# Transposing a gated product by DMA in two 16-bit planes, and moving two modulation streams to the output stages

## The chip, the cores and the metric

The kernel runs on one core of one Trainium2 chip. The metric is the device time of one execution in microseconds (us); the time before is the median of three runs. The profile is of one execution of its own, and its span is a little shorter than the time of a run.

## The reference

A backbone of two layers over 256 latent tokens and 256 context tokens, each of width 1024, in float32. Each layer is a half-step feed-forward network (FFN), a token mixer (neighbourhood attention in layer 0, a short gated convolution in layer 1) and a second half-step FFN; after each the stream is normalised. A modulation vector per sub-layer (shift, scale, gate) comes from the conditioning vector and a wide weight, `ada_w`. What matters here:

```python
def swiglu_ffn(h, w_in, w_out):
    a, u = jnp.split(h @ w_in, 2, axis=-1)
    return (jax.nn.silu(a) * u) @ w_out

def half_step_ffn(x, shift, scale, gate, w_in, w_out, g, b):
    y = swiglu_ffn(modulate(x, shift, scale), w_in, w_out)
    return post_norm_update(x, y, gate, 0.5, g, b)

m = (s_c @ ada_w[i] + ada_b[i]).reshape(B, N_MOD, 1, D)
```

`w_in` is 1024 x 5632, `w_out` is 2816 x 1024 and each of the nine vectors of a layer takes a 1024 x 1024 slice of `ada_w` (4.2 MB).

## The kernel before

**Precision.** Every float32 operand is split in two parts that TensorE reads as fp32r: ACT copies it (the high part, names that end in h) and DVE subtracts (the low part, names that end in l). A product is three matmuls: high by high, high by low, low by high (lines 160 to 167). So each weight tile costs ACT two copies of 128x512 and DVE two subtractions before TensorE (PE) can use it (`parts`, lines 207 to 214).

**The later FFNs.** The first FFN, which also takes the context tokens, has code of its own. The other three, (0,1), (1,0) and (1,1), go through `ffn` (line 825), and only the 256 latent tokens are left, in two tiles t of 128. Each FFN has two stages:

- The input stage (`panels`, line 449) has 11 panels p of 256 + 256 columns of `w_in` (the part for silu and the factor), 4 weight units per panel, each of 2 x 128 rows by 512 columns, and 2 token tiles: 88 steps of the generator. I call such a step a chunk: it is 6 matmuls of 128x512. When the last unit of a panel and a token tile is done, `done` in `gated` (line 476) runs: ACT takes the silu out of PSUM (line 478), DVE multiplies by the factor (line 479) into a tile that is called sil.
- The output stage (`out_gemm`, line 520) multiplies the transposed product by `w_out`: 2 halves n of the columns, 11 units and 2 token tiles, so 44 chunks. `order_skew` (line 493) runs token tile 1 five units behind tile 0, so five weight units are held between the two; the last FFN uses `order_last`.

**The transposition.** The output stage needs the product with the FFN's columns on the partitions. Four chunks (`G_LAG`) after a panel's second token tile, `rest` (line 482) puts four TensorE transposes of 128x128 into a PSUM bank called gT (line 487), and `finish` splits the bank into gh and gl.

**What sets the order.** TensorE runs in the order in which the program writes its instructions. `Late` (line 120) holds a function back until a number of chunks has passed, or until its value is asked for. On ACT, DVE, SP and POOL a scheduler places each instruction by a priority (its place in the program, less an offset; weight loads are 40 places ahead); each engine then runs its list strictly in order. SP issues nearly all DMAs, in one queue.

**Weight buffers.** A unit needs a raw tile (4 buffers) and a high and a low tile (5 buffers, and with `ext[0] = 3` three more, `whx` and `wlx`): eight in rotation. A buffer is free again when PE has used the unit for both token tiles.

**Background.** `stream` and `ada` (line 275) make the modulation vectors bit by bit: 16 loads of 512 KB for two vectors (tiles called ar, line 303), each followed by two DVE accumulations of 128x512 (acc, lines 294 and 296), then a bias, four small matmuls (line 327) and a store. `tick` (line 143) runs `rate` steps per chunk; `set_background(gen, rate, hold)` starts them `hold` chunks late, and `drain` runs what is left at once. The streams for the vectors (1,4) and (1,5) run beside the input stage of FFN (0,1) at 0.35 a chunk, those for (1,6) and (1,7) beside that of FFN (1,0) at 0.25, and (1,8) beside that of FFN (1,1) at 0.15.

Of the kernel before, what the change touches and what calls it, by code (L numbers as in the profile page):

```python
# [8 lines left out]

F32 = mybir.dt.float32  # L10
F32R = mybir.dt.float32r
AF = mybir.ActivationFunctionType
ALU = mybir.AluOpType
AX = mybir.AxisListType
# [2 lines left out]
P = 128  # L17
# [34 lines left out]
LT_LAG = (5, 5)  # L52
F0_LAG = (5, 5, 6, 7)
G_LAG = 4
ROPE_EARLY = 70
S_EARLY = 40
V_LAG = 1
# [6 lines left out]
ZP = ((0, 0), (1, 0), (0, 1), (0, 2), (1, 1), (1, 2))  # L64
E0 = (0,)
E2 = (0, 5, 7)
HOLD = 20


@with_exitstack  # L70
def backbone_kernel(
# [6 lines left out]
    nc = tc.nc  # L78
    sync = nc.sync
# [4 lines left out]
    sp = ctx.enter_context(tc.tile_pool(name="sp", bufs=2))  # L84
# [10 lines left out]
    def nm(s):  # L95
        uid[0] += 1
        return f"{s}_{uid[0]}"
# [370 lines left out]
    def run(gen):  # L468
        for _ in gen:
            pass  # L470

    def gated(func, finish, s):

        part, res = {}, []

        def done(p, t, bk):
            g = sp.tile([P, 256], F32, tag="s2", bufs=S2, name=nm("sil"))
            nc.scalar.activation(g, bk[:, 0:256], func)
            gate_ins[:] = [nc.vector.tensor_tensor(out=g, in0=g, in1=bk[:, 256:512], op=ALU.mult)]
            part[p, t] = g  # L480
            if t == 1:
                def rest():
                    ps = tpb(s)
                    for i in range(2):
                        g = part.pop((p, i))
                        for j in range(2):
                            nc.tensor.transpose(ps[:, j * 256 + i * P:j * 256 + (i + 1) * P], g[:, j * P:(j + 1) * P], ident)  # L487
                    return finish(p, ps)
                res.append(Late(G_LAG, rest))

        return done, res
# [330 lines left out]
            return hi[:, s:s + P], lo[:, s:s + P]  # L822
        return f

    def ffn(hTs, later, l, j, i, gm, nxt, own=()):
# [5 lines left out]
        done, gT = gated(AF.Silu, finish, "gT")  # L831
# [7 lines left out]
        drain()  # L839
# [278 lines left out]
    srow = cp.tile([24, P], F32, tag="row", name="srow")  # L1118
# [52 lines left out]

    cols = [(0, 256), (512, 768)] + [(D + n * 256, 2 * D + n * 256) for n in range(4)]
    run(panels(cols, w, hTs, lead_in(6), done, "wc"))
    g, hTs, later = sub_end(sc_w_out[0], lhs_T(yT), KC, 1, 1, 5, 1.0, (1, 6), "wo", order_late(KU))
    run(g)
    set_background(stream([(1, 8, 0)]), 0.15)
# [55 lines left out]
```

## Time and profile before

| | |
|---|---|
| time, median of 3 runs | 1262.23 us (1261.55 to 1262.94) |
| span of the profiled execution | 1259.9 us |
| PE busy | 1245.4 us, 99% |
| DVE busy | 952.5 us, 76% |
| ACT busy | 589.9 us, 47% |
| DMA | 268.6 MB, mean 213 GB/s |

The profile lists engines, groups of instructions and waits; L164 is line 164 of the kernel above. PE is TensorE's matmuls, DVE is VectorE, ACT is ScalarE, SP the engine whose queue issues DMAs. In a row of a timeline the first number is the start in us from the beginning of the span, the second how long the row's instructions took together, and xN their number; what ended the engine's idle time stands in brackets. A row of the windows has the stretch in us, the busy time of each engine with its instructions, the granted clock of TensorE (1.00 is full), the busy share of the 16 DMA engines and what they moved in GB/s.

### The profile page before, as it was taken

How to read it: one execution, taken by the hardware profiler on the slowest of the kernel's cores; microseconds unless marked ns; L12 is line 12 of the kernel's file. 1: busy time of each engine (PE TensorE's matmuls, PEld its weight loads, DVE VectorE, ACT ScalarE, POOL GpSimd, SP SyncE). 2: the span in 40 equal slices, each digit the busy share in tenths (PEclk: the TensorE clock that was granted, in tenths of full speed). 3: DMA queues.
4: the chain of work that ended last, by engine and by line, in shares of the span. 5: the costliest groups of instructions: out<-in, count | busy, mean ns of one | idle time of the engine just before them, and what ended most of it. 6: DMA issues, size and time to landing. Idle time of an engine off the chain costs nothing.

```text
span 1259.9 us, 17303 instructions
## 1 busy us (share of the span) xinstructions
PE 1245.4 (99%) x5922; PEld 1007.2 (80%) x5922; DVE 952.5 (76%) x1678; ACT 589.9 (47%) x1152; POOL 41.4 (3%) x71
## 2 busy tenths in 40 slices
PE   9999999999999999999999999999999999999997
PEld 6787778777878877877888788888788887888786
DVE  3699987888878877889898546988546788876546
ACT  2432132312326456687655435655435644655431
POOL 0000000000001011121000000000000000000000
PEclk9999999999999999999999999999999999999999
DMA  9976678878842744465899645898645764886641
GB/s 300 310 241 215 197 239 280 269 255 266 300 149 85 217 93 92 93 130 170 256 342 318 225 144 169 285 340 268 214 145 170 247 202 131 262 289 184 223 158 55
DMA packets 202776, 268.59 MB, mean 213 GB/s; under 512 B 30090, under 2 KB 149362, under 8 KB 202688
## 3 DMA queue, kind: packets, MB, share of 16 engines
q1 hardware_dynamic: 202652, 267.48, 67.3%
q8 instruction: 46, 0.75, 0.2%
q14 instruction: 42, 0.34, 0.1%
q10 hardware_dynamic: 36, 0.02, 0.0%
HBM read 265.27 MB, written 2.17 MB: 212 GB/s over the span
## 4 chain that ended last, share of the span: by engine, by line
PE 92%; DVE 3%; ACT 3%; issue 1%; DMA 0%; POOL 0%; DVEq 0%; SPq 0%; ACTq 0%; POOLq 0%
PE f L679 19%; PE w L164 17%; PE w L167 17%; PE w L165 17%; PE wkv L164 2%; PE wkv L165 2%; PE wkv L167 2%; PE wc L164 2%; PE wc L167 2%; PE wc L165 2%; PE gT L487 1%; PE ada L608 1%; PE ada L327 1%; PE S L971 1%; ACT pr L979 1%
## 5 line engine op out<-in xcount | busy, mean ns | idle before, releaser
L210 ACT ACTIVATE w1h<-w1r 128x512 fp32r<-128x512 f32 (+1 forms) x352 | 199.8, 620 | 180.4 <-DMA w1r<-in_ffn_w_in_dram 73.3
L213 DVE TENSOR_TENSOR w1l<-w1r,w1h 128x512 fp32r<-128x512 f32 (+1 forms) x352 | 222.9, 679 | 44.6 <-ACT w1h L210 43.3
L164 PE MATMUL w<-w1h,hTh 128*128 128x512 f32 x528 | 209.4, 397 | 0.9 <-ACT hTh L112 0.9
L165 PE MATMUL w<-w1l,hTh 128*128 128x512 f32 x528 | 206.0, 390 | 0.2 <-DVE w1l L213 0.2
L296 DVE SCALAR_TENSOR_TENSOR acc<-ar,cst,acc 128x512 f32<-128x512 f32 x266 | 186.0, 746 | 15.4 <-DMA ar<-in_ada_w_dram 15.4
L164 PE MATMUL w<-w2h,gh 128*128 128x512 f32 (+1 forms) x446 | 173.4, 389 | 0.0
L165 PE MATMUL w<-w2l,gh 128*128 128x512 f32 (+1 forms) x446 | 172.1, 386 | 0.0
L213 DVE TENSOR_TENSOR w2l<-w2r,w2h 128x512 fp32r<-128x512 f32 x176 | 114.3, 688 | 76.0 <-ACT w2h L210 75.2
L210 ACT ACTIVATE w2h<-w2r 128x512 fp32r<-128x512 f32 x176 | 101.6, 624 | 146.0 <-PE w L167 103.6
L167 PE MATMUL w<-w1h,hTl 128*128 128x512 f32 x528 | 163.2, 390 | 0.3 <-DVE hTl L113 0.2
L167 PE MATMUL w<-w2h,gl 128*128 128x512 f32 (+1 forms) x446 | 136.1, 386 | 0.0
L679 PE MATMUL f<-h0h,w1h 128*128 128x512 f32 x352 | 133.3, 394 | 0.4 <-DVE h0h L634 0.4
L679 PE MATMUL f<-h0l,w1h 128*128 128x512 f32 x352 | 133.2, 391 | 0.0
L679 PE MATMUL f<-h0h,w1l 128*128 128x512 f32 x352 | 132.7, 390 | 0.0
L164 PEld LDWEIGHTS w<-w1h,hTh 128*128 128x128 f32 x528 | 99.2, 188 | 23.8 <-ACT hTh L112 1.7
L167 PEld LDWEIGHTS w<-w1h,hTl 128*128 128x128 f32 x528 | 98.9, 188 | 22.4 <-DVE hTl L113 1.5
L165 PEld LDWEIGHTS w<-w1l,hTh 128*128 128x128 f32 x528 | 99.2, 188 | 20.2 <-DVE w1l L213 0.6
L164 PEld LDWEIGHTS w<-w2h,gh 128*128 128x128 f32 x446 | 83.8, 188 | 19.2 <-issue 1.7
L165 PEld LDWEIGHTS w<-w2l,gh 128*128 128x128 f32 x446 | 83.8, 188 | 16.6
L167 PEld LDWEIGHTS w<-w2h,gl 128*128 128x128 f32 x446 | 83.3, 188 | 17.1
L679 PEld LDWEIGHTS f<-h0h,w1h 128*128 128x128 f32 x352 | 65.9, 189 | 18.8 <-issue 4.2
L679 PEld LDWEIGHTS f<-h0l,w1h 128*128 128x128 f32 x352 | 65.6, 188 | 14.3 <-issue 0.6
(186 smaller groups left out, 1684.5 us busy)
## 6 DMA issues: line engine op xcount, KB each, us to landing
w1r<-in_ffn_w_in_dram SPq DMA_DIRECT2D x340, 256.0 KB
ar<-in_ada_w_dram SPq DMA_DIRECT2D x128, 512.0 KB
w2r<-in_ffn_w_out_dram SPq DMA_DIRECT2D x88, 512.0 KB
ar<-in_ada_w_dram SPq DMA_DIRECT2D x32, 256.0 KB
wkvr<-in_na_w_qkv_dram SPq DMA_DIRECT2D x32, 256.0 KB
wcr<-in_sc_w_in_dram SPq DMA_DIRECT2D x32, 256.0 KB
wqr<-in_na_w_qkv_dram SPq DMA_DIRECT2D x8, 512.0 KB
wor<-in_na_w_out_dram SPq DMA_DIRECT2D x8, 512.0 KB
```

The costliest lines, as they stand in the source:

```text
L164: nc.tensor.matmul(ps, lh, rh, start=first and i == 0, stop=False)
L165: nc.tensor.matmul(ps, lh, rl, start=False, stop=False)
L167: nc.tensor.matmul(ps, ll, rh, start=False, stop=last and i == n - 1)
L210: nc.scalar.activation(hi[:, a:a + m // W_HI], raw[:, a:a + m // W_HI], AF.Copy)
L213: nc.vector.tensor_tensor(out=lo[:, a:b], in0=raw[:, a:b], in1=hi[:, a:b].bitcast(F32), op=ALU.subtract)
L296: nc.vector.scalar_tensor_tensor(out=a, in0=src, scalar=sc, in1=a, op0=ALU.mult, op1=ALU.add)
L327: nc.tensor.matmul(ps[32 * j:32 * j + 32, :], ones, acc[i][h], start=True, stop=True)
L487: nc.tensor.transpose(ps[:, j * 256 + i * P:j * 256 + (i + 1) * P], g[:, j * P:(j + 1) * P], ident)
L608: nc.tensor.matmul(ps[o:o + 32, 0:m], cst[:, a * kt + i, :], w[:, i, j, :], start=(a == 0 and i < 2), stop=(a == last and i >= kt - 2))
L679: nc.tensor.matmul(ps, w, hT0[k][part == 1], start=(k == part == 0), stop=(k == KC - 1 and part == 1))
L971: nc.tensor.matmul(banks[i], (qh, qh, ql)[f][ps, qs], (kh, kl, kh)[f][ps, :], start=f == 0, stop=f == 2)
L979: nc.scalar.activation(pr, S, AF.Exp, bias=mx[:, 0:1], accum_out=mx[:, 1:2])
```

## The change

In the three later FFNs (`gated(..., by_dma=True)`) the product is no longer transposed on TensorE. Per panel:

- For each token tile ACT reads the 128x256 float32 product as 512 numbers of 16 bits and writes them apart, into a tile `hal` of two planes of 128x256 (the low and the high halves of the words; 4 buffers). Six chunks later in the program (`T_LAG`) SP issues one DMA that transposes both planes, 128x512 of 16 bits, into `halT`, which is shared by the two token tiles (2 buffers).
- Eight more chunks later (`D_LAG`) `joined` lets ACT put the two planes of the panel together again into a float32 tile `gTw` (one copy of 128x1024 numbers of 16 bits), and `finish` splits that tile into gh and gl, from SBUF now and not from PSUM.

To make room, `ext[0]` goes from 3 to 2: seven weight buffers in rotation where there were eight. The two streams of FFN (0,1) and FFN (1,0) are held back 92 chunks, so past the 88 of the input stage, into the output stage; the first at 0.55 a chunk, the second at 0.3, and what the program has left of the second by then comes beside the convolution's input stage. The drains behind the input stages of these two FFNs go (the last argument of `ffn`); one stands behind FFN (0,1) instead, and one behind the convolution's panels.

```diff
+D_LAG = 8
+T_LAG = 6
-HOLD = 20
+HOLD = 92
...
-    ext[0] = 3
-    set_background(stream([(1, 4, 0), (1, 5, 0)]), 0.35, HOLD)
-    hTs, later = ffn(hTs, later, 0, 1, 2, 8, (1, 0), own)
-    set_background(stream([(1, 6, 0), (1, 7, 0)]), 0.25)
-    hTs, later = ffn(hTs, later, 1, 0, 0, 2, (1, 3))
+    ext[0] = 2
+    set_background(stream([(1, 4, 0), (1, 5, 0)]), 0.55, HOLD)
+    hTs, later = ffn(hTs, later, 0, 1, 2, 8, (1, 0), own, False)
+    drain()
+    set_background(stream([(1, 6, 0), (1, 7, 0)]), 0.3, HOLD)
+    hTs, later = ffn(hTs, later, 1, 0, 0, 2, (1, 3), (), False)
...
         def done(p, t, bk):
             g = sp.tile([P, 256], F32, tag="s2", bufs=S2, name=nm("sil"))
             nc.scalar.activation(g, bk[:, 0:256], func)
             gate_ins[:] = [nc.vector.tensor_tensor(out=g, in0=g, in1=bk[:, 256:512], op=ALU.mult)]
+            if by_dma:
+                if t == 0:
+                    part[p] = hp.tile([P, 4, 256], U16, tag="halT", bufs=2, name=nm("halT"))
+                halves = hp.tile([P, 2, 256], U16, tag="hal", bufs=4, name=nm("hal"))
+                nc.scalar.activation(halves, g.bitcast(U16).rearrange("p (f s) -> p s f", s=2), AF.Copy)
+                turn = Late(T_LAG, lambda: sync.dma_start_transpose(part[p][:, :, t * P:(t + 1) * P],
+                                                                    halves.rearrange("p s f -> p (s f)")))
+                turns.append(turn)
+                if t == 1:
+                    mine = turns[-2:]
+                    def joined():
+                        for turn in mine:
+                            turn.get()
+                        w = sp.tile([P, 512], F32, tag="tmp", bufs=3, name=nm("gTw"))
+                        nc.scalar.activation(w.bitcast(U16).rearrange("p (f s) -> p s f", s=2),
+                                             part.pop(p).rearrange("p (s j) n -> p s (j n)", s=2), AF.Copy)
+                        return finish(p, w)
+                    res.append(Late(T_LAG + D_LAG, joined))
+                return
```

**ACT in the input stage of FFN (0,1)**, one panel in the middle. First the kernel before, from the silu of one panel's token tiles to that of the next; the two w1h in a row are the two halves of one weight unit:

```order
L478 ACTIVATE sil_1219_6509<-w1_1202_6420 128x256
L478 ACTIVATE sil_1221_6522<-w1_1205_6432 128x256
L210 ACTIVATE w1h_1261_6723<-w1r_1260_6722 128x512 x2
L210 ACTIVATE w1h_1266_6750<-w1r_1265_6749 128x512 x2
L112 ACTIVATE gh_1232_6572<-gT_1231_6567 128x512
L210 ACTIVATE w1h_1271_6773<-w1r_1270_6772 128x512 x2
L210 ACTIVATE w1h_1277_6803<-w1r_1276_6802 128x512 x2
L478 ACTIVATE sil_1241_6622<-w1_1225_6534 128x256
```

The same engine and stage of the changed kernel (its L481, L213 and L115 are L478, L210 and L112 before; L487 and L498 are new):

```order
L481 ACTIVATE sil_1243_6588<-w1_1229_6509 128x256
L487 ACTIVATE hal_1245_6592<-sil_1243_6588 128x512
L481 ACTIVATE sil_1246_6600<-w1_1230_6516 128x256
L213 ACTIVATE w1h_1279_6756<-w1r_1278_6755 128x512 x2
L487 ACTIVATE hal_1247_6603<-sil_1246_6600 128x512
L213 ACTIVATE w1h_1285_6784<-w1r_1284_6783 128x512 x2
L498 ACTIVATE gTw_1281_6770<-halT_1244_6591 128x2x512
L115 ACTIVATE gh_1282_6772<-gTw_1281_6770 128x512
L213 ACTIVATE w1h_1293_6816<-w1r_1292_6815 128x512 x2
L213 ACTIVATE w1h_1298_6839<-w1r_1297_6838 128x512 x2
L481 ACTIVATE sil_1265_6693<-w1_1251_6614 128x256
```

The two planes (hal) and the joining (gTw) of a panel have come into ACT's list, and the joining stands one weight unit behind the plane that its DMA reads: what follows on ACT waits for that DMA.

**SP at the end of that input stage** of the changed kernel; halT_1288 and halT_1310 are the last two panels, w2r the units of the output stage, ar the stream:

```order
L208 DMA w2r_1336_7008<-in_ffn_w_out_dram 128x2x512
L488 DMA_TRANSPOSE halT_1288_6801<-hal_1289_6802 128x4x128
L488 DMA_TRANSPOSE halT_1288_6801<-hal_1291_6813 128x4x128
L208 DMA w2r_1343_7038<-in_ffn_w_out_dram 128x2x512
L208 DMA w2r_1348_7063<-in_ffn_w_out_dram 128x2x512
L208 DMA w2r_1352_7087<-in_ffn_w_out_dram 128x2x512
L208 DMA w2r_1359_7117<-in_ffn_w_out_dram 128x2x512
L488 DMA_TRANSPOSE halT_1310_6906<-hal_1311_6907 128x4x128
L488 DMA_TRANSPOSE halT_1310_6906<-hal_1313_6918 128x4x128
L208 DMA w2r_1364_7145<-in_ffn_w_out_dram 128x2x512
L306 DMA ar_1355_7101<-in_ada_w_dram 128x1024
L306 DMA ar_1362_7131<-in_ada_w_dram 128x1024
```

Each panel's two transposing DMAs have come into the queue between the weight loads, and the loads of the stream now stand between those of the output stage; three of them (ar_1341, ar_1346 and ar_1351) stand some hundred rows earlier.

**DVE in the output stage of FFN (0,1).** The kernel before, from the eighth unit's low part on:

```order
L213 TENSOR_TENSOR w2l_1338_7099<-w2r_1336_7097,w2h_1337_7098 128x512 x2
L113 TENSOR_TENSOR gl_1320_7018<-gT_1318_7012,gh_1319_7017 128x512
...
L213 TENSOR_TENSOR w2l_1341_7119<-w2r_1339_7117,w2h_1340_7118 128x512 x2
L213 TENSOR_TENSOR w2l_1344_7139<-w2r_1342_7137,w2h_1343_7138 128x512 x2
L213 TENSOR_TENSOR w2l_1347_7159<-w2r_1345_7157,w2h_1346_7158 128x512 x2
L213 TENSOR_TENSOR w2l_1352_7184<-w2r_1350_7182,w2h_1351_7183 128x512 x2
```

The changed kernel, from the same unit's low part on (its L216 is L213 before, its L297 and L299 are L294 and L296):

```order
L216 TENSOR_TENSOR w2l_1350_7065<-w2r_1348_7063,w2h_1349_7064 128x512 x2
L299 SCALAR_TENSOR_TENSOR acc_1347_7054<-ar_1363_7141,cst_89,acc_1347_7054 128x512 x2
L216 TENSOR_TENSOR w2l_1354_7089<-w2r_1352_7087,w2h_1353_7088 128x512 x2
L299 SCALAR_TENSOR_TENSOR acc_1347_7054<-ar_1369_7170,cst_89,acc_1347_7054 128x512 x2
L299 SCALAR_TENSOR_TENSOR acc_1347_7054<-ar_1374_7195,cst_89,acc_1347_7054 128x512
L216 TENSOR_TENSOR w2l_1361_7119<-w2r_1359_7117,w2h_1360_7118 128x512 x2
L299 SCALAR_TENSOR_TENSOR acc_1347_7054<-ar_1374_7195,cst_89,acc_1347_7054 128x512
L297 TENSOR_SCALAR acc_1383_7245<-ar_1378_7219,cst_89 128x512
L216 TENSOR_TENSOR w2l_1366_7147<-w2r_1364_7145,w2h_1365_7146 128x512 x2
```

Two or three accumulations now stand between the low parts of two successive units, which stood alone before. Between the eighth unit's low part and the 21st's there are 22 accumulations in all and six instructions of the residual and its statistics. The output stage of FFN (1,0) has its accumulations in the same places, also to the end of the stage, although the program spreads it at 0.3 a chunk.

More of the change, by code (lines that the diff above doesn't have):

```diff
@@ L11 @@
 F32R = mybir.dt.float32r
+U16 = mybir.dt.uint16
 AF = mybir.ActivationFunctionType
@@ L470, in run, with gated @@
             pass
-    def gated(func, finish, s):
-        part, res = {}, []
+    def gated(func, finish, s, by_dma=False):
+        part, res, turns = {}, [], []
         def done(p, t, bk):
@@ L823, in lhs_T, with ffn @@
         return f
-    def ffn(hTs, later, l, j, i, gm, nxt, own=()):
+    def ffn(hTs, later, l, j, i, gm, nxt, own=(), made_here=True):
         def finish(p, ps):
@@ L829, in finish @@
             return hi, lo
-        done, gT = gated(AF.Silu, finish, "gT")
+        done, gT = gated(AF.Silu, finish, "gT", True)
         def done2(p, t, bk):
@@ L838, in ffn @@
         run(panels([(p * 256, FF + p * 256) for p in range(NP)], ffn_w_in[l, j], hTs, lead_in(NP), done2, "w1", own))
-        drain()
+        if made_here:
+            drain()
         g, hTs, later = sub_end(ffn_w_out[l, j], lhs_T(gT), 2 * NP, l, i, gm, 0.5, nxt, "w2",
@@ L1108, in backbone_kernel @@
     bias_rows.clear()
[L1109 to L1115 removed]
+    ext[0] = 2
+    set_background(stream([(1, 4, 0), (1, 5, 0)]), 0.55, HOLD)
+    hTs, later = ffn(hTs, later, 0, 1, 2, 8, (1, 0), own, False)
+    drain()
+    set_background(stream([(1, 6, 0), (1, 7, 0)]), 0.3, HOLD)
+    hTs, later = ffn(hTs, later, 1, 0, 0, 2, (1, 3), (), False)
     srow = cp.tile([24, P], F32, tag="row", name="srow")
@@ L1173, in backbone_kernel @@
     run(panels(cols, w, hTs, lead_in(6), done, "wc"))
+    drain()
     g, hTs, later = sub_end(sc_w_out[0], lhs_T(yT), KC, 1, 1, 5, 1.0, (1, 6), "wo", order_late(KU))
```

## The prediction

> **What bounds the kernel now.** First the page: the span, the engines' busy time and the chain that ended last.
>
> ```profile
> span 1259.9 us, 17303 instructions
> PE 1245.4 (99%) x5922; PEld 1007.2 (80%) x5922; DVE 952.5 (76%) x1678; ACT 589.9 (47%) x1152; POOL 41.4 (3%) x71
> PE 92%; DVE 3%; ACT 3%; issue 1%; DMA 0%; POOL 0%; DVEq 0%; SPq 0%; ACTq 0%; POOLq 0%
> ```
>
> TensorE carries 92% of the chain. Whether anything but TensorE limits the stages that change is read from the windows: the input stages of FFN (0,1) and (1,0) and the output stage of (0,1), without their edges.
>
> ```profile
> 605.00:713.00 108.00, 108.00 (x499) 88.43 (x499) 89.66 (x153) 57.80 (x111) 0.00 (x0) 1.00 0.87 291
> 719.90:780.00 60.10, 60.10 (x271) 49.40 (x270) 32.94 (x56) 24.32 (x45) 1.08 (x2) 1.00 0.51 166
> 800.00:896.00 96.00, 96.00 (x442) 79.30 (x440) 78.56 (x133) 50.05 (x95) 0.00 (x0) 1.00 0.88 291
> ```
>
> TensorE never stops in them, at clock 1.00. In the input stages DVE is busy 83% and the DMA engines 87%; the output stage has room. As busy matmuls may still be slow ones, the third view is TensorE's timeline round one transposition.
>
> ```profile
> 611.18 0.62 PE L167 MATMUL w<-w1h,hTl 128*128 128x512 f32 x2
> 611.63 0.60 PE L487 MATMUL gT<-ident,sil 128*128 128x128 f32 x4
> 611.99 0.48 PE L164 MATMUL w<-w1h,hTh 128*128 128x512 f32 x1
> ...
> 613.46 0.40 PE L164 MATMUL w<-w1h,hTh 128*128 128x512 f32 x1
> ...
> 614.84 0.39 PE L164 MATMUL w<-w1h,hTh 128*128 128x512 f32 x1
> ...
> 616.20 0.39 PE L164 MATMUL w<-w1h,hTh 128*128 128x512 f32 x1
> ```
>
> A chunk of six matmuls takes 616.20 - 614.84 = 1.36 us; the chunk with the transposes takes 613.46 - 611.63 = 1.83. So four transposes cost 0.47 us of a TensorE that has no idle time.
>
> **The transposes go.** The tile gT shows how many there are.
>
> ```profile
> L487 PE MATMUL gT<-ident,sil x132: 270/272/273, 611.6 to 1196.3; 128*128 128x128 f32 x132
> ```
>
> 132 / 4 = 33 groups at 0.47 us are 15.5 us. (The 272 ns of one overlap, so 132 x 0.272 would be too much.) More than this can't be won, since TensorE waits for nothing in these stages.
>
> **ACT gets two planes and a joining per panel.** Its timeline over one panel of FFN (1,0), and the groups that price the new instructions:
>
> ```profile
> 850.86 0.38 ACT L478 ACTIVATE sil<-w 128x256 f32<-128x256 f32 x1 [0.98 <-PE w L167]
> 851.14 1.14 ACT L210 ACTIVATE w1h<-w1r 128x512 fp32r<-128x512 f32 x2
> 853.62 1.15 ACT L210 ACTIVATE w1h<-w1r 128x512 fp32r<-128x512 f32 x2 [1.34 <-issue]
> 855.37 0.60 ACT L112 ACTIVATE gh<-gT 128x512 fp32r<-128x512 f32 x1 [0.60 <-PE gT L487]
> 856.77 1.15 ACT L210 ACTIVATE w1h<-w1r 128x512 fp32r<-128x512 f32 x2 [0.79 <-PE w L167]
> 859.49 1.15 ACT L210 ACTIVATE w1h<-w1r 128x512 fp32r<-128x512 f32 x2 [1.57 <-PE w L167]
> 860.85 0.38 ACT L478 ACTIVATE sil<-w 128x256 f32<-128x256 f32 x1 [0.21 <-PE w L167]
> L210 ACT ACTIVATE w1h<-w1r 128x512 fp32r<-128x512 f32 x336 | 192.4, 625 | 177.4 <-DMA w1r<-in_ffn_w_in_dram 70.3 <-PE w L167 52.4 <-issue 32.7
> L112 ACT ACTIVATE oT<-osum 128x256 fp32r<-128x256 f32 x8 | 3.3, 411 | 1.4 <-DVE osum L1015 1.4
> ```
>
> A copy of 256 costs 411 ns and one of 512 costs 625, so another 512 add 214 x 2 = 428: I put a plane (512 numbers) at 0.62 us and the joining (1024) at 1.05. No row has 16-bit numbers; at half that speed a panel would take 2 x 0.43 + 0.86 = 1.7 us more, and the points below for L would lie that much lower. ACT's list for a panel is then four weight units at 1.15, two silus at 0.38, two planes, the joining and gh at 0.60, plus one wait of about 0.5 for DVE's product (0.42, below) between silu and plane: 4.6 + 0.76 + 1.24 + 1.05 + 0.60 + 0.5 = 8.75 us. TensorE gives it 8 x 1.36 = 10.9.
>
> The remainder has to cover the wait for the DMA. The joining stands one weight unit (1.15 us) behind the second plane, so a DMA that lands L us after that plane holds ACT for L - 1.15, and ACT keeps pace while 8.75 + L - 1.15 stays under 10.9: **L up to 3.3 us is free**. Behind the waiting joining stand the copies of the next weight units, and TensorE needs those. It has a lead: with seven buffers a unit is converted six units of 2.72 us ahead, 16.3, less 1.95 for the conversion (below), less some 1.8 by which the joining comes after its buffer's release: 12.6 us. So TensorE first stops when 11 x (L - 3.3) exceeds 12.6, at L = 4.45, and the gain is gone at L = 4.8.
>
> No row shows a transposing DMA. Three rows bound L: the small DMAs of the attention's bias, from the chain of waits and SP's timeline, and the DMA engines' windows.
>
> ```profile
> 549.15 5.13 DMA bias<-in_na_rpb_dram
> 547.81 1.95 SPq L879 DMA_DIRECT2D bias<-in_na_rpb_dram  x3
> 0.73 2.13 SPq L582 DMA_DIRECT2D ar<-in_ada_w_dram  x4
> 4.18 1.61 PE L608 MATMUL ada<-ar,cst 128*32 128x128 f32 x16 [0.27 <-ACT cst L259]
> DMA packets 501, 0.12 MB, mean 31 GB/s; under 512 B 501, under 2 KB 501, under 8 KB 501
> q1 hardware_dynamic: 501, 0.12, 47.3%
> DMA packets 2928, 3.29 MB, mean 329 GB/s; under 512 B 185, under 2 KB 2773, under 8 KB 2928
> ```
>
> The upper bound is a bias DMA's 5.13 us. The lower is the program's first load: issued at 0.73, used by 4.18, so at most 3.45. An issue takes SP 1.95 / 3 = 0.65. The transfer is 131 KB: 0.4 us at 329 GB/s (the 10 us from 1100 on), or, if each 256-byte row of a plane is a packet like the bias's (501 packets in the 4 us from 446 on, 0.473 x 16 x 4 / 501 = 60 ns each), 512 x 60 / 16 = 1.9 us. I take L = 3.5, near the lower bound, since the queue is short here: a panel's weights are 2.1 MB, 6.4 us at 329 GB/s, and two transfers bring 0.8 to 3.8 more, 7.2 to 10.2 of 10.9. ACT then falls back 11 x 0.2 = 2 us per stage, inside the lead: **0 us**. Moving the streams out of these stages is what leaves the DMA engines that room. SP's eight weight issues and two new ones at 0.65 fit easily.
>
> **The streams in the output stages.** DVE's rows there, and its accumulations:
>
> ```profile
> 733.68 1.29 DVE L213 TENSOR_TENSOR w2l<-w2r,w2h 128x512 fp32r<-128x512 f32 x2 [1.45 <-ACT w2h L210]
> 733.02 1.15 ACT L210 ACTIVATE w2h<-w2r 128x512 fp32r<-128x512 f32 x2 [1.59 <-PE w L167]
> 735.74 1.15 ACT L210 ACTIVATE w2h<-w2r 128x512 fp32r<-128x512 f32 x2 [1.57 <-PE w L167]
> 862.62 0.42 DVE L479 TENSOR_TENSOR sil<-sil,w 128x256 f32<-128x256 f32 x1 [0.85 <-ACT sil L478]
> 862.96 2.73 DVE L296 SCALAR_TENSOR_TENSOR acc<-ar,cst,acc 128x512 f32<-128x512 f32 x4
> L391 DVE SCALAR_TENSOR_TENSOR x<-x,res 128x512 f32<-128x512 f32 x18 | 12.4, 687 | 0.3
> ```
>
> A unit comes every 2.72 us (735.74 - 733.02), and its low part is ready 733.68 + 1.29 - 733.02 = 1.95 us after a buffer comes free. Token tile 1 holds five units, so eight buffers leave a conversion 5.4 us and seven leave 2.72: a margin of 0.8. DVE has 2.72 - 1.29 = 1.4 us free per unit, room for two accumulations of 0.68. From the eighth to the 21st unit it has 14 x 1.29 + 22 x 0.68 + 6 x 0.69 = 37.2 us to do in 14 x 2.72 = 38.1, and where three accumulations stand together, or the residual's steps, a low part comes 0.6 to 1.3 us late against that margin. I count 0.8 us for each of two output stages: **+1.6 us** (0 if all fits, up to 5.1 each if a stream's load lands a bias DMA too late and DVE waits in line).
>
> At the start of each of the three FFNs the first plane stands in ACT's list ahead of the last high part of the new hT, with its 0.5 us wait: 0 to 1.1 us each, but TensorE uses that part two chunks after the first, so I take 0.2: **+0.6 us**. The split from SBUF costs what it cost from PSUM, and the lost eighth buffer nothing in the input stages, where the lead is long.
>
> **Sum.** 1259.9 - 15.5 + 0 + 1.6 + 0.6 = 1246.6; the median run lies 1262.2 - 1259.9 = 2.3 above the profiled span, so **1248.9 us**.
>
> **Rivals.** *The joining waits for slow DMAs (slower).* With L at the upper bound of 5.13 each stage loses 1.83 x 11 - 12.6 = 7.5 us, three stages 22.5: **1271 us**. It decides from L = 4.8. For it: the waiting engine is the one that converts the weights, and two DMAs per panel share a queue with loads of 512 KB. Against it: the first plane is sent 1.4 us before the second, and nothing else queues then. The Trainium skill, "VectorE: DVE Perf Modes", speaks for it: The three transpose paths gives 1309 ns for a 128x128 tile of 16 bits by DMA, and Rules for kernel authors sends such tiles to TensorE where PSUM will do; four of these in a row would be an estimated 5.2 us with no landing, past the point. No row here shows that.
>
> *The output stages run out of DMA.* 22 + 16 loads of 0.524 MB are 19.9 MB, 60.6 us at 329 GB/s, in 44 x 1.36 = 59.8 us, and four transposing DMAs bring 1.6 to 7.6: 2.4 to 8.4 us late per stage, in the middle 5.4, twice: **1259.7 us**. For it: DVE and SP wait in order behind these loads. Against it: three of the 16 loads are issued long before, and six units are loaded ahead.
>
> *The removal frees nothing* (**1262 us**): TensorE would have to be held by something hidden. The 0.47 us, in plain sight, speaks against it.
>
> **Chances.** Forecast 0.60; slow DMAs 0.23; output stages 0.13, of which 0.06 still faster, 0.05 the same and 0.02 slower; nothing freed and mishaps 0.04, half same and half slower. About 0.2%, 2.5 us, is what a measurement can tell. Of the slow DMAs 0.01 falls within that. Faster 0.60 + 0.06 = 0.66; same 0.05 + 0.02 + 0.01 = 0.08; slower 0.22 + 0.02 + 0.02 = 0.26. The forecast's own range is 1246.7 (no new wait) to 1255. The whole range goes from 1246.5 to 1270: it takes in the starved output stages and about half of the slow DMAs.
>
> **What would show it.** Right: no gT on TensorE, input stages with PE as dense as now, 11 x 0.47 = 5 us shorter each; joinings whose wait on halT is about 2.3 us; L of 3 to 4.4 from plane to joining; TensorE's waits for w2l some tenths each, under 2 us per output stage. Wrong: TensorE waiting for w1h in the later panels (slow DMAs), or w2r and ar as the longest waits of ACT and DVE in the output stages.

## The result, and the profile after

| | before | after |
|---|---|---|
| time, median of 4 runs each | 1262.07 us (1261.55 to 1262.94) | 1289.97 us (1287.89 to 1293.83) |
| span of the profiled execution | 1259.9 us | 1287.0 us |
| ratio after to before, 95% interval | | 1.0225 (1.0212 to 1.0239) |

The change makes the kernel 2.2% slower. The forecast was 1248.9 us and its range ended at 1270. From the page of the changed kernel, the span, the engines and the chain that ended last:

```profile
span 1287.0 us, 17240 instructions
PE 1241.4 (96%) x5790; PEld 997.5 (78%) x5790; DVE 948.6 (74%) x1678; ACT 659.3 (51%) x1251; POOL 40.9 (3%) x71
PE 64%; DMA 11%; DVE 10%; ACT 8%; issue 4%; SPq 2%; POOL 0%; DVEq 0%; ACTq 0%
```

PE has 132 matmuls fewer, as it should. But its share of the chain falls from 92% to 64%: DMA, DVE and ACT now decide when work ends. The windows of the changed kernel show where: the input stage of FFN (0,1), the first 15 us of its output stage, the next 17, and the start of the last output stage.

```profile
605.00:713.00 108.00, 108.00 (x478) 89.41 (x478) 68.09 (x117) 75.33 (x137) 0.00 (x0) 1.00 0.84 229
713.00:728.00 15.00, 14.54 (x62) 10.88 (x61) 9.69 (x18) 8.98 (x17) 0.00 (x0) 1.00 0.81 212
728.00:745.00 17.00, 9.91 (x31) 7.35 (x30) 13.35 (x25) 5.60 (x9) 0.00 (x0) 0.70 0.91 309
1209.00:1234.00 25.00, 15.44 (x49) 11.24 (x48) 8.42 (x15) 10.68 (x18) 0.00 (x0) 0.80 0.85 212
```

The input stage is as dense as before: PE 108.00 of 108.00. TensorE stops only when the output stage has begun, 7.1 us in one stretch of 17 and 9.6 in one of 25. There its granted clock falls as well, to 0.70 and 0.80.

**How the lag builds up.** ACT's timeline over one panel of FFN (0,1), from one silu of the second token tile to the next:

```profile
689.15 0.37 ACT L481 ACTIVATE sil<-w 128x256 f32<-128x256 f32 x1
689.41 1.14 ACT L213 ACTIVATE w1h<-w1r 128x512 fp32r<-128x512 f32 x2
690.45 0.62 ACT L487 ACTIVATE hal<-sil 128x512 uint16<-128x512 uint16 x1
690.97 1.14 ACT L213 ACTIVATE w1h<-w1r 128x512 fp32r<-128x512 f32 x2
695.05 1.36 ACT L498 ACTIVATE gTw<-halT 128x1024 uint16<-128x1024 uint16 x1 [2.94 <-DMA halT<-hal]
...
701.12 0.37 ACT L481 ACTIVATE sil<-w 128x256 f32<-128x256 f32 x1
```

The second plane is ready at 690.45 + 0.62 = 691.07, and the joining starts at 695.05. So L, the time from the plane to the landing of its transposing DMA, is 3.98 us; one weight unit covers part of it, and ACT stands for 2.94. SP's timeline splits L: its two transposing issues end at 689.27 + 3.02 = 692.29.

```profile
689.27 3.02 SPq L488 DMA_TRANSPOSE halT<-hal  x2
```

So about 1.2 us are the issue and 2.8 the rest, up to the start of the joining. The groups of the new instructions (shortest, median and longest in ns) and the waits of the whole run (in all, times, longest, in us):

```profile
L498 ACT ACTIVATE gTw<-halT x33: 1340/1366/1371, 614.6 to 1226.3; 128x1024 uint16<-128x1024 uint16 x33
L487 ACT ACTIVATE hal<-sil x66: 613/630/670, 603.4 to 1218.0; 128x512 uint16<-128x512 uint16 x66
L488 SPq DMA_TRANSPOSE halT<-hal x66: 1188/1190/1995, 604.1 to 1218.8; - x66
```

```profile
ACT gTw L498 <- DMA halT<-hal: 81.7, 30, 7.7
ACT hal L487 <- DVE sil L482: 32.2, 28, 1.8
PE w L167 <- ACT w2h L213: 16.8, 5, 7.1
PE w L168 <- DVE w2l L216: 10.2, 6, 4.8
```

30 of the 33 joinings wait for their DMA, 81.7 us together, and 28 planes wait 1.15 us on average for DVE's product. TensorE does not wait for ACT in the input stage, where weights are converted well ahead. But ACT gets later. The next rows show the last panel's second silu before the change, and then the last panel after it on TensorE and on ACT.

```profile
719.88 0.38 ACT L478 ACTIVATE sil<-w 128x256 f32<-128x256 f32 x1 [0.98 <-PE w L167]
```

```profile
714.30 0.61 PE L170 MATMUL w<-w1h,hTl 128*128 128x512 f32 x2
731.50 0.53 PE L167 MATMUL w<-w2h,gh 128*128 128x512 f32 x1 [2.71 <-ACT w2h L213]
736.42 0.79 PE L168 MATMUL w<-w2l,gh 128*128 128x512 f32 x1 [4.38 <-DVE w2l L216]
```

```profile
723.96 0.37 ACT L481 ACTIVATE sil<-w 128x256 f32<-128x256 f32 x1
...
725.26 0.62 ACT L487 ACTIVATE hal<-sil 128x512 uint16<-128x512 uint16 x1
728.93 1.34 ACT L498 ACTIVATE gTw<-halT 128x1024 uint16<-128x1024 uint16 x1 [3.04 <-DMA halT<-hal]
730.30 0.63 ACT L115 ACTIVATE gh<-gTw 128x512 fp32r<-128x512 f32 x1
730.84 2.17 ACT L213 ACTIVATE w2h<-w2r 128x512 fp32r<-128x512 f32 x4
```

Before, this silu started when PE let it (0.98 us waited for PE). After, PE ended the panel at 714.30 + 0.61 = 714.91 and the silu came at 723.96: ACT is **9.05 us late**. In the last three panels it had taken (723.96 - 689.15) / 3 = 11.60 us a panel, TensorE 8 x 1.36 = 10.88. Counting back by 10.88 a panel, ACT was 689.15 - 682.27 = 6.9 us late three panels earlier and 608.87 - 606.11 = 2.8 after the first panel. The kernel before is 2.8 us late after the first panel too, but from the fifth panel on it is not late at all.

**Where it is paid.** Behind the last plane the order gives ACT the joining first and only then the weights of the output stage. So ACT waits 3.04 us for the DMA, the next w2h starts at 730.84, and TensorE has stopped. That is the first stop, 2.71 us. The second, 4.38 us, is the stream's: on DVE four accumulations stand ahead of the low part from 732.57 on, the first of them held 0.91 us for its load, and SP is busy issuing such loads. It takes the lag as well: in the kernel that moves only the streams (experiment 1) no wait for a low part is longer than 1.0 us.

```profile
732.57 1.41 DVE L299 SCALAR_TENSOR_TENSOR acc<-ar,cst,acc 128x512 f32<-128x512 f32 x2 [0.91 <-DMA ar<-in_ada_w_dram]
...
735.68 1.28 DVE L216 TENSOR_TENSOR w2l<-w2r,w2h 128x512 fp32r<-128x512 f32 x2
```

```profile
727.82 8.29 SPq L306 DMA_DIRECT2D ar<-in_ada_w_dram  x5
```

The last FFN has no stream in its output stage, and TensorE still stops for 25.00 - 15.44 = 9.6 us in the window above. PE's and ACT's timelines there:

```profile
1204.50 0.62 PE L170 MATMUL w<-w1h,hTl 128*128 128x512 f32 x2
...
1212.72 0.50 PE L167 MATMUL w<-w2h,gh 128*128 128x512 f32 x1 [2.17 <-ACT w2h L213]
...
1228.92 0.79 PE L167 MATMUL w<-w2h,gh 128*128 128x512 f32 x1 [7.15 <-ACT w2h L213]
```

```profile
1216.71 0.37 ACT L481 ACTIVATE sil<-w 128x256 f32<-128x256 f32 x1
...
1218.01 0.62 ACT L487 ACTIVATE hal<-sil 128x512 uint16<-128x512 uint16 x1
1226.35 1.34 ACT L498 ACTIVATE gTw<-halT 128x1024 uint16<-128x1024 uint16 x1 [7.71 <-DMA halT<-hal]
```

TensorE ended the input stage at 1204.50 + 0.62 = 1205.12. ACT is 1216.71 - 1205.12 = 11.6 us late, the last joining waits 7.71 us, and TensorE stops for 2.17 and for 7.15. The window right behind the shorter stop shows TensorE's clock:

```profile
1212.70:1216.00 3.30, 3.05 (x7) 2.25 (x8) 3.30 (x6) 2.32 (x5) 0.00 (x0) 0.56 0.95 252
```

### The profile page after: what moved, and what is told of

The parts are those of the page before. It is cut to its first block, busy times and chain, and to the rows that moved or that the text cites. A ratio compares the mean times of both kernels' runs of the same rounds, so it can differ in the third digit from the quotient of the medians.

```text
span 1287.0 us, 17240 instructions
## 1 busy us (share of the span) xinstructions
PE 1241.4 (96%) x5790; PEld 997.5 (78%) x5790; DVE 948.6 (74%) x1678; ACT 659.3 (51%) x1251; POOL 40.9 (3%) x71
## 3 DMA queue, kind: packets, MB, share of 16 engines
HBM read 265.27 MB, written 2.17 MB: 208 GB/s over the span
## 4 chain that ended last, share of the span: by engine, by line
PE 64%; DMA 11%; DVE 10%; ACT 8%; issue 4%; SPq 2%; POOL 0%; DVEq 0%; ACTq 0%
PE f L702 18%; PE w L168 10%; PE w L167 10%; PE w L170 10%; DVE w1l L216 4%; DMA halT<-hal 4%; DMA ar<-in_ada_w_dram 3%; DMA w1r<-in_ffn_w_in_dram 2%; PE wc L167 2%; PE wc L168 2%; PE wc L170 2%; DVE w2l L216 2%; ACT w1h L213 1%; PE wkv L167 1%; ACT hal L487 1%
## 5 line engine op out<-in xcount | busy, mean ns | idle before, releaser
L216 DVE TENSOR_TENSOR w1l<-w1r,w1h 128x512 fp32r<-128x512 f32 (+1 forms) x352 | 223.1, 679 | 34.4 <-ACT w1h L213 32.6
L213 ACT ACTIVATE w1h<-w1r 128x512 fp32r<-128x512 f32 (+1 forms) x352 | 197.7, 617 | 87.4 <-PE w L170 25.6
L167 PE MATMUL w<-w1h,hTh 128*128 128x512 f32 x528 | 206.0, 390 | 0.9 <-ACT hTh L115 0.9
L299 DVE SCALAR_TENSOR_TENSOR acc<-ar,cst,acc 128x512 f32<-128x512 f32 x266 | 186.6, 746 | 19.7 <-DMA ar<-in_ada_w_dram 19.5
L167 PE MATMUL w<-w2h,gh 128*128 128x512 f32 (+1 forms) x446 | 177.1, 398 | 16.9 <-ACT w2h L213 16.8
L168 PE MATMUL w<-w2l,gh 128*128 128x512 f32 (+1 forms) x446 | 177.0, 397 | 10.2 <-DVE w2l L216 10.2
L213 ACT ACTIVATE w2h<-w2r 128x512 fp32r<-128x512 f32 x176 | 100.4, 622 | 122.0 <-PE w L170 91.2
L216 DVE TENSOR_TENSOR w2l<-w2r,w2h 128x512 fp32r<-128x512 f32 x176 | 113.6, 686 | 31.0 <-ACT w2h L213 30.4
L116 DVE TENSOR_TENSOR gl<-gTw,gh 128x512 fp32r<-128x512 f32 x33 | 22.8, 691 | 88.5 <-ACT gh L115 88.5
L498 ACT ACTIVATE gTw<-halT 128x1024 uint16<-128x1024 uint16 x33 | 44.9, 1362 | 81.7 <-DMA halT<-hal 81.7
```

Source lines behind the costliest of these rows:

```text
L116: return a, nc.vector.tensor_tensor(out=lo, in0=src, in1=hi.bitcast(F32), op=ALU.subtract)
L167: nc.tensor.matmul(ps, lh, rh, start=first and i == 0, stop=False)
L168: nc.tensor.matmul(ps, lh, rl, start=False, stop=False)
L213: nc.scalar.activation(hi[:, a:a + m // W_HI], raw[:, a:a + m // W_HI], AF.Copy)
L216: nc.vector.tensor_tensor(out=lo[:, a:b], in0=raw[:, a:b], in1=hi[:, a:b].bitcast(F32), op=ALU.subtract)
L299: nc.vector.scalar_tensor_tensor(out=a, in0=src, scalar=sc, in1=a, op0=ALU.mult, op1=ALU.add)
```

## The experiments

**The theories.** A: ACT's joinings wait in order for the transposing DMAs; ACT falls behind TensorE in each input stage and the output stage pays. B: the streams in the output stages cost the time. C: ACT's new work is too much even without the wait. D and T3 came up on the way. D: the DMA engines have no room for planes and streams together. T3: the lost eighth buffer costs time. The time before was 1261.8 to 1262.1 us in each of the four sets of runs.

| kernel | us, median | ratio to before, 95% interval |
|---|---|---|
| streams only | 1270.35 | 1.0069 (1.0054 to 1.0084) |
| seven buffers only | 1261.59 | 1.0000 (0.9990 to 1.0009) |
| DMA transposes only | 1299.39 | 1.0299 (1.0284 to 1.0314) |
| joining without the wait | 1257.62 | 0.9963 (0.9949 to 0.9977) |
| later joining | 1258.57 | 0.9972 (0.9956 to 0.9988) |
| later joining, again | 1259.67 | 0.9977 (0.9967 to 0.9987) |
| last three panels by DMA | 1268.52 | 1.0055 (1.0037 to 1.0074) |
| first eight panels by DMA | 1279.19 | 1.0132 (1.0109 to 1.0156) |
| later joining, streams back | 1268.76 | 1.0061 (1.0044 to 1.0078) |
| later joining, streams spread | 1262.83 | 1.0006 (0.9996 to 1.0017) |
| the same, held 60 chunks | 1259.18 | 0.9979 (0.9968 to 0.9990) |
| later joining, streams one by one | 1250.60 | 0.9910 (0.9893 to 0.9926) |

**1. Streams only.** The changed kernel with the transposes on TensorE:

```diff
-        done, gT = gated(AF.Silu, finish, "gT", True)
+        done, gT = gated(AF.Silu, finish, "gT")
```

> The transposes stay on TensorE; only the streams move to the output stages and the eighth weight buffer goes. Theory A (ACT's joinings, which wait in order for the transposing DMAs, cost the 43 us that lie between the forecast's 1247 and the measured 1290): all of the loss is in the other half of the change, so 1262 to 1266 us, PE stalls in the output stages under 2 us each. Rival B (the streams in the output stages cost it: their loads and accumulations stand ahead of the weights' low parts): the two stages that hold streams keep their 24 us, so about 1286 us.

1270.35 us: 8.2 above before. Neither theory had the size, but A is much nearer: B asked for 1286. The windows of the input and the output stage of FFN (0,1), and DVE's timeline at one stop:

```profile
605.00:713.00 108.00, 108.00 (x497) 89.37 (x496) 70.64 (x119) 57.81 (x110) 0.00 (x0) 1.00 0.67 210
713.00:780.00 67.00, 64.35 (x280) 50.49 (x283) 52.93 (x90) 25.73 (x46) 0.80 (x2) 1.00 0.83 289
```

```profile
742.01 1.41 DVE L299 SCALAR_TENSOR_TENSOR acc<-ar,cst,acc 128x512 f32<-128x512 f32 x2 [1.85 <-DMA ar<-in_ada_w_dram]
743.34 0.68 DVE L216 TENSOR_TENSOR w2l<-w2r,w2h 128x512 fp32r<-128x512 f32 x1
```

The output stage loses 67.00 - 64.35 = 2.7 us, in stops of a microsecond or less: an accumulation waits for its load, and the low part that TensorE needs stands behind it. In the output stage of FFN (1,0), from 896 to 960 us, it is 64.00 - 61.16 = 2.8.

**2. Seven buffers only.** The kernel before with one line changed:

```diff
-    ext[0] = 3
+    ext[0] = 2
```

> The kernel before with seven weight buffers instead of eight, nothing else. Theory A and the forecast: 1262 to 1264 us, the streams' place costs the 8 us of streams_only. Rival T3 (the lost buffer costs them): 1270 us.

1261.59 us, no difference. So T3 is out: the 8.2 us come with the place of the streams, not with the buffer alone. Whether an eighth buffer would help the streams in the output stages, or the planes, was not run.

**3. DMA transposes only.** The changed kernel with hold, rates and drains of the streams as before.

```diff
-HOLD = 92
+HOLD = 20
...
-    set_background(stream([(1, 4, 0), (1, 5, 0)]), 0.55, HOLD)
-    hTs, later = ffn(hTs, later, 0, 1, 2, 8, (1, 0), own, False)
-    drain()
+    set_background(stream([(1, 4, 0), (1, 5, 0)]), 0.35, HOLD)
+    hTs, later = ffn(hTs, later, 0, 1, 2, 8, (1, 0), own)
...
```

> The streams go back to the input stages at their old rates; planes, transposing DMAs and joinings stay, with seven buffers. Theory A: the loss stays, 1283 to 1295 us, with stalls of about 12 us at the start of each of the three output stages (more DMA traffic beside the transposing DMAs could make it worse). Rival B: the two output stages with streams recover their 24 us, about 1266 us, and only the last FFN still loses.

1299.39 us, 9 slower than the whole change and above A's range too. B is out. Put as before, the streams cost more beside the planes than in the output stages; numbers 8 and 12 come back to this.

**4. Joining without the wait.**

```diff
...
-                halves = hp.tile([P, 2, 256], U16, tag="hal", bufs=4, name=nm("hal"))
...
+                halT, hal = part[p]
+                halves = hal[:, t]
...
-                                             part.pop(p).rearrange("p (s j) n -> p s (j n)", s=2), AF.Copy)
+                                             part.pop(p)[1], AF.Copy)
```

> The joining reads the untransposed planes, so that it waits for no DMA; all DMAs are still issued, but nothing reads what they write. ACT's work is the same. Theory A: per panel ACT then needs 4.6 + 0.76 + 1.24 + 1.37 + 0.63 + 1.15 (wait for the product) = 9.75 us of 10.9, keeps up, and nearly all of the 43 us goes: 1247 to 1253 us. Rival B: the streams' stalls stay, 1270 to 1280 us. Rival C (ACT's added work by itself is too much for it, not the wait): stalls stay at the start of the output stages, 1275 us or more.

1257.62 us: 32.4 of the loss go with the wait alone. This kernel leaves the transposition out, so it shows only what the wait costs. The time is above A's 1247 to 1253, which had no room for the 8.2 us of the streams. C is out. Only times are read for this kernel, no profile.

**5. Later joining.** The joining keeps its wait but is held behind the newest weight conversion that the program has asked for (`queued`), and the program asks for it four chunks later.

```diff
-D_LAG = 8
+D_LAG = 12
...
-                nc.scalar.activation(hi[:, a:a + m // W_HI], raw[:, a:a + m // W_HI], AF.Copy)
+                last_hi[:] = [nc.scalar.activation(hi[:, a:a + m // W_HI], raw[:, a:a + m // W_HI], AF.Copy)]
...
-                        nc.scalar.activation(w.bitcast(U16).rearrange("p (f s) -> p s f", s=2),
+                        with queued(last_hi):
+                          nc.scalar.activation(w.bitcast(U16).rearrange("p (f s) -> p s f", s=2),
```

> The same work, but the joining is held behind the newest weight conversion that the program has asked for 18 chunks after the panel: two weight units (2.3 us) instead of one stand between the second plane and the joining, and behind the last panel five units of the output stage instead of none. Theory A: the wait of 2 to 3 us per joining is covered by that work, ACT's cycle falls to about 10 us of 10.9, and the time to 1247 to 1256 us. Rival B: no change there, 1280 to 1290 us. Rival C: no change, 1280 to 1290 us.

1258.57 us: 31.4 faster than the changed kernel and 0.3% faster than the one before, with the same work. The wait of this kernel's joinings, to be held against 81.7 us and 30 times:

```profile
ACT gTw L501 <- DMA halT<-hal: 17.4, 16, 2.9
```

The lag tells the same. Read like that of the changed kernel, it grows to 6 or 7 us in the first panels, but at the end of the three input stages it is 0.2 us, where the changed kernel has 9.0, 10.6 and 11.6. A holds, though the time is 2.6 us above its range, which again left the streams' 8.2 out. What TensorE wins by the 33 groups is now to be seen: the busy time of PE in the pages of streams only and of this kernel, both without the big stops.

```profile
PE 1248.3 (98%) x5922; PEld 1004.6 (79%) x5922; DVE 953.2 (75%) x1678; ACT 592.6 (47%) x1152; POOL 42.6 (3%) x71
```

```profile
PE 1233.7 (98%) x5790; PEld 993.0 (79%) x5790; DVE 950.2 (76%) x1678; ACT 661.6 (53%) x1251; POOL 41.0 (3%) x71
```

1248.3 - 1233.7 = 14.6 us. (The kernel before has 1245.4 for the same 5922 matmuls as streams only, which would make it 11.7; the figure is good to some 3 us.) With that the change adds up as 1262.1 - 14.6 + 8.2 (streams) + 34.3 = 1290.0, where the 34.3 are a remainder; experiments 4 and 5 took 32.4 and 31.4 of them away.

**6 and 7. Does the lag build up over the panels, or do the last three joinings do it alone?** Some panels of each FFN by DMA, the others on TensorE:

```diff
-            if by_dma:
+            if by_dma and p >= NP - 3:
```

> Only the last three panels of each FFN go by DMA, the first eight are transposed on TensorE; the streams stay in the output stages. The sum so far: streams only 1270.4; 24 of the 99 transposing groups... put plainly, 9 groups of 33 no longer on TensorE win 9 x 0.44 = 4 us (0.44 us per group from the 14.6 us of PE that the 33 groups take); the waits of all joinings cost the changed kernel 1290 - 1270.4 + 14.6 = 34 us. Theory A1 (each joining's wait adds to a lag that is built up over eleven panels): three panels build up too little to use up the lead, 1266 to 1270 us. Theory A2 (the lead is gone at the start of the output stage anyway, and what counts is the last panels' joinings, which stand ahead of the weights that TensorE needs next): the 34 us stay, 1290 to 1305 us.

```diff
-            if by_dma:
+            if by_dma and p < NP - 3:
```

> The reverse: the first eight panels go by DMA, the last three are transposed on TensorE. 24 groups win 24 x 0.44 = 10.6 us. Theory A1: eight of eleven panels' lag is left when the output stage starts, so most of the 34 us stays, 1275 to 1290 us. Theory A2: nearly all of the 34 us goes, and 1270.4 - 10.6 gives 1258 to 1263 us.

1268.52 and 1279.19 us, both where A1 put them. Three joinings at the end, in the same place ahead of the same weights, cost some 2 us: 1270.35 - 9 x 0.44 = 1266.4 was the sum without a wait. Eight panels early in the stage cost 1279.2 - (1270.35 - 10.6) = 19.4. Here the lag shows within the input stage and by a wait that the changed kernel does not have: TensorE's first own transposes wait for a late product, once in each FFN and 11.7 us in all (the row is from the last FFN):

```profile
1185.98 1.12 PE L510 MATMUL gT<-ident,sil 128*128 128x128 f32 x4 [5.66 <-DVE sil L482]
```

**8. Later joining, streams back** in the input stages, as in number 3:

> The later joining, and the streams back in the input stages. Theory A: the streams' 8 us in the output stages go, the transposes' 14.6 us are won, 1247 to 1250 us. Rival D (the input stages' DMA engines, 87% busy before, have no room for streams and transposing DMAs together, so weights or planes come late whatever ACT's order is): 1262 us or more, with ACT waiting for w1r or halT within the input stages.

1268.76 us. The forecast of A alone is wrong by 20 us, and the time is where D has it. This kernel's windows of the two input stages, and ACT's waits in the first of them for weights that are still on their way, in the kernel before and in this one:

```profile
605.00:713.00 108.00, 105.95 (x468) 85.79 (x467) 83.68 (x143) 71.80 (x128) 0.00 (x0) 1.00 0.90 274
800.00:896.00 96.00, 92.52 (x396) 73.04 (x394) 69.53 (x117) 58.29 (x104) 0.00 (x0) 1.00 0.83 261
```

```profile
ACT w1h L210 <- DMA w1r<-in_ffn_w_in_dram: 13.5, 10, 3.8
ACT w1h L215 <- DMA w1r<-in_ffn_w_in_dram: 27.3, 13, 6.0
```

The weights come late, as D has it, and TensorE is idle 2.1 and 3.5 us in these windows. D's reason is not shown. By shares there is too little room: before, weights and streams took 0.87 of the DMA engines in this stage, and the planes add 0.84 - 0.67 = 0.17 (the changed kernel's window less that of streams only, neither with a stream there), 1.04 in all by this estimate. But the engines are busy only 0.90 and 0.83 here, and number 12 moves more in both windows without a stop.

**9 to 11. The streams spread over both stages.** The later joining once more, and beside it two ways to spread (the first is spread_a in the expectations):

> The kernel with the later joining once more, with more rounds, beside the two below. From the parts: 1262.1 - 14.6 (transposes off TensorE) + 8.2 (streams in the output stages) = 1255.7 us if the waits for the transposing DMAs are gone; more than that by what is left of them. Expected 1255 to 1259 us.

```diff
-HOLD = 92
+HOLD = 20
...
-    set_background(stream([(1, 4, 0), (1, 5, 0)]), 0.55, HOLD)
+    set_background(stream([(1, 4, 0), (1, 5, 0)]), 0.2, HOLD)
...
-    set_background(stream([(1, 6, 0), (1, 7, 0)]), 0.3, HOLD)
+    set_background(stream([(1, 6, 0), (1, 7, 0)]), 0.15, HOLD)
```

> The later joining, with the two streams spread over both stages of their FFN (20 chunks held, 0.2 and 0.15 steps a chunk). Theory A and D together (each stage has room for about half the stream: the output stage loses about 4 us where DVE and the DMA engines carry the whole stream, the input stage loses where they carry the whole stream and the planes): 1249 to 1254 us. Rival: any stream beside the planes makes the input stage late, 1260 us or more.

The other way has a hold of 60 and rates of 0.3 and 0.2:

> The same with the streams held 60 chunks, at 0.3 and 0.2 steps a chunk, so that they begin in the last third of the input stage. Theory A and D: between the other two, 1251 to 1257 us; the rival: as spread_a, since the last panels get stream loads and planes together, 1260 us or more.

1259.67, 1262.83 and 1259.18 us: no gain from spreading, against expectation; the rival's 1260 or more came true for the first spread kernel only. In that kernel one stop at the start of the output stage stands out, on PE, DVE and SP:

```profile
731.12 0.80 PE L170 MATMUL w<-w2l,gh 128*128 128x512 f32 x1 [4.41 <-DVE w2l L218]
```

```profile
728.60 0.75 DVE L301 SCALAR_TENSOR_TENSOR acc<-ar,cst,acc 128x512 f32<-128x512 f32 x1 [3.75 <-DMA ar<-in_ada_w_dram]
```

```profile
722.07 8.40 SPq L308 DMA_DIRECT2D ar<-in_ada_w_dram  x4
```

Four stream loads stand together in SP's list and take it 8.4 us, DVE waits 3.75 us in line for one of them, and TensorE stops 4.41 for the low part behind; the same stop in FFN (1,0) is 3.81. The program asks for one load every five chunks, but the scheduler bunches what the program spreads.

**12. Streams one by one.** Both streams at 0.18 a chunk from chunk 20, each load held behind the newest weight load and each accumulation behind the newest low part:

```diff
-                sync.dma_start(w, ada_w[l, k * P:(k + 1) * P, m * D:(m + 1) * D])
+                with queued(last_ld if pinned else ()):
+                  sync.dma_start(w, ada_w[l, k * P:(k + 1) * P, m * D:(m + 1) * D])
...
-                for i in gate_ins:
+                for i in gate_ins + (last_lo if pinned else []):
...
```

> The later joining, with both streams spread over their FFNs (20 chunks held, 0.18 steps a chunk) and each stream load and accumulation held behind the newest weight load and the newest low part, so that they come one by one and not in bunches (the spread kernel without this stops TensorE 4.6 and 4.0 us, once per output stage, behind a bunch of four loads and six accumulations). Theory: with neither ACT waiting for planes nor DVE for bunched loads, what is left is 1262.1 - 14.6 = 1247.5 us and the FFN starts: 1248 to 1253 us. Rival (a stream beside the planes costs DMA time wherever it is put): 1257 us or more.

1250.60 us, 0.9910 (0.9893 to 0.9926) of the time before: the fastest of all, with every vector made and every panel transposed by DMA. Its span, the two stages of FFN (0,1) and the input stage of FFN (1,0), and ACT's wait for weights from 605 to 713:

```profile
span 1248.7 us, 17208 instructions
```

```profile
605.00:713.00 108.00, 108.00 (x478) 89.42 (x477) 78.00 (x135) 76.05 (x137) 0.00 (x0) 1.00 0.97 286
713.00:780.00 67.00, 66.54 (x299) 53.44 (x298) 52.13 (x88) 38.84 (x71) 1.07 (x2) 1.00 0.76 236
800.00:896.00 96.00, 96.00 (x425) 79.49 (x424) 69.03 (x121) 69.57 (x123) 0.00 (x0) 1.00 0.95 289
```

```profile
ACT w1h L215 <- DMA w1r<-in_ffn_w_in_dram: 12.2, 8, 3.1
```

The input stages are dense with the DMA engines 97% and 95% busy, and the output stage loses half a microsecond where the changed kernel had lost 0.46 + 7.09 us by 745. So the rivals of 9 to 12 fall, and so does D's reason: with loads and accumulations bunched (the first spread kernel, at nearly the same rates) the time is 1262.83, one by one it is 1250.60. ACT ends the three input stages 5.0, 3.6 and 0.2 us late here, and TensorE does not stop: so a lag of 5 us costs nothing with the joining placed later. Loads and accumulations were not held apart from each other, and streams one by one in the output stages alone were not run.

## Why the prediction was wrong, step by step

- **The transposes, -15.5 us.** Right but for the size: -14.6 by the busy time of PE (number 5), which is good to some 3 us.
- **ACT's list of 8.75 us a panel.** Too short. The plane was right (0.62; 0.63 measured). The joining takes 1.37, not 1.05; the bound for 16 bits, half the speed, would have been 1.91 for it and 1.05 for a plane, further off. The wait for DVE's product, once in most panels, is 1.15 us, not 0.5. With gh at 0.63 the list is 4.6 + 0.76 + 1.26 + 1.37 + 0.63 + 1.15 = 9.77. Counted the prediction's way, L was then free up to 10.88 - 9.77 + 1.15 = 2.3 and not up to 3.3.
- **L = 3.5 us.** About right: 3.98 in the panel shown, 728.93 - 725.88 = 3.05 at the end of FFN (0,1), and from 3.0 to 4.3 in 27 of the 30 joinings that waited. At the end of the last FFN it was 1226.35 - 1218.63 = 7.7, above the upper bound of 5.13. The Trainium skill, "VectorE: DVE Perf Modes", The three transpose paths, gave an estimated 5.2 us for four tiles in a row. The trace has less than that in 28 of the 30 and more in two. SP's issue takes 1.19 us, not 0.65.
- **The step that failed** is "ACT then falls back 11 x 0.2 = 2 us per stage, inside the lead: 0 us". Both halves are wrong. ACT falls back by 11.60 - 10.88 = 0.7 us a panel late in the stage, and ends 9 to 11.6 us late. And the lead of 12.6 us is that of the input stage; it does not carry over whole. In the output stage five of the seven buffers are held for token tile 1, and the prediction's own figure for what is left there is 0.8 us, which it used for the streams and not for ACT. That the held buffers shorten the lead is an argument, as no run has the planes with more buffers, and the figure of 0.8 is too small for this place: experiment 12, with the joining later, carries a lag of 5.0 us over without a stop. What the runs show is that a lag of 9 us or more, which never stopped TensorE in the stage where it arose (PE 108.00 of 108.00), was collected, with the last joining's wait on top, at the next stage's start: 34 us in three FFNs, of which 32.4 go when the joining does not wait and 31.4 when it stands later.
- **What the lag costs beyond the stop.** Before, the granted clock was 1.00 in every window shown; behind the stops it was 0.70 and 0.80 in the windows shown. The prediction had no term for this. Two pages of the profile give its size. For the same 5790 matmuls PE is busy 1241.4 - 1233.7 = 7.7 us longer in the changed kernel than in the one with the later joining (span 1257.0). Its idle time is 1287.0 - 1241.4 = 45.6 us against 1257.0 - 1233.7 = 23.3, so 22.3 more. Of the 30.0 us between the two spans about a quarter is thus slow matmuls and the rest is stops. The Trainium skill, "TensorE: Matmul & The Clock Gate", Part 1: The HAM clock gate, says that the clock falls to a half after an idle window of about 3.4 us. In the trace a shorter stop was enough: the clock is 0.56 in the 3.3 us behind the stop of 2.17 us.
- **The streams, +1.6 us.** Too small: +8.2. What was missing is the order: loads and accumulations stand in bunches ahead of low parts, and DVE waits in line for loads. Experiment 12 shows that the streams can be had for some 3 us at most (1250.6 against 1262.1 - 14.6), but spread over both stages; that they fit into the output stages alone, as counted, is not shown.
- **The lost buffer, 0 us.** Right, alone (experiment 2).
- **The rivals.** "The joining waits for slow DMAs" named the mechanism. It had L = 4.8 as the point from which it decides, and 22.5 us at L = 5.13; L of 3 to 4 was enough for 34, and the stops came at w2h, not at w1h in the later panels, as it had them. "The output stages run out of DMA" is part of the 8.2 us: DVE waits for ar there, as foreseen.
- **The room on the DMA engines.** The prediction said that moving the streams out is what makes room for the planes. Experiments 3 and 8 show that streams put as before make it worse, but experiment 12 has the planes and 12 of a stream's 16 loads in the input stage of FFN (0,1) without a stop. Order decided, not room.
- **The signs.** Three signs of being right came true although the time did not: no gT on TensorE, dense input stages, L of 3 to 4.4 in most panels. Of the signs of being wrong, waits of TensorE for w1h did not come. What told were TensorE's waits at the start of the output stages: for w2l, which were to be some tenths of a microsecond and are up to 4.8, and above all for w2h, which no sign named.

Not settled: why the last landing of the last FFN took 7.7 us. The DMA engines were full when that DMA was issued (the windows give a busy share of 1.02 from 1218 to 1220, against 0.82 from 724 to 726 in FFN (0,1)), so it may have stood behind weight loads; this was not tried apart.

## What to carry to other kernels

A wait of an engine that is far from busy (ACT was at 51%) still costs when its list is in order and the weights stand behind it: compare its cycle, waits included, with the pace of the bound engine, and carry the lag on to the next stage, with that stage's margin and not with the lead of the stage where it arose. Before giving up such a change, move the waiting instruction a few units down the list: the same work went from 1290 to 1259 us. And look in the order, not in the program's rates, for bunches of background work: held one by one behind the work that matters, the same streams cost some 3 us at most.

## What the runs showed of the hardware

- A transposing DMA of 128x512 numbers of 16 bits from SBUF to SBUF costs SP 1.19 us to issue, 3.0 to 4.3 us from data to the start of its reader beside weight loads (27 of 30), and by an estimate (0.84 - 0.67) x 108 / 20 = 0.9 us of all 16 DMA engines (ten panels in the window, two DMAs each): 131 KB / 0.9 us = 145 GB/s, where the weights move at 210 / 0.67 = 313.
- An ACT copy of 1024 numbers of 16 bits that interleaves two planes takes 1.37 us; one of 512 that parts them takes 0.63.
- Behind a stop of TensorE of 2.17 us its granted clock was 0.56 over 3.3 us.
